# Storing the last two result tiles of a batched 64x64 matmul whole and in halves, instead of in halves and quarters

## The chip, the cores and the metric

One core of one Trainium2 chip. The metric is device time in microseconds (us), the median of the fast runs of a kernel. A core has a matrix engine (PE), a vector engine (DVE), a scalar engine (ACT), POOL and SP, which both mostly issue transfers here, and 16 transfer (DMA) engines that all issuers share.

## The reference

1024 independent products of 64x64 float32 matrices; 32 MB are read, 16 MB are written.

```python
def setup_inputs():
    return {
        "a": np.random.randn(1024, 64, 64).astype(np.float32),
        "b": np.random.randn(1024, 64, 64).astype(np.float32),
    }

def reference(a, b):
    return np.matmul(a, b).astype(np.float32)
```

## The kernel before

Sixteen steps t of 64 matrices each. A step casts b to bf16, spreads a's transposed blocks into a block-diagonal tile, multiplies into PSUM, copies the result to a 1 MB tile `o_sb` (128 partitions x 8 KB) and stores it. POOL issues all stores. The parts that matter, cut:

```python
n_t, n_s = B // 64, B // 128
HOLD = 2
o_v = out.rearrange("(t gh x) (mo w) n -> t (x mo) gh (w n)", gh=8, x=8, w=4)
o_pool = ctx.enter_context(tc.tile_pool(name="o_pool", bufs=8))
...
def store(t):
    for piece in held.pop(t):
        piece()

def multiply(t):
    ...
    last = t == n_t - 1
    o_sb = o_pool.tile([128, 8, 2, 2, 64], fp32, name="o_sb")

    def put(lo, n):                      # n of 8 parts: 8 is 1 MB, 4 is 512 KB, 2 is 256 KB
        nc.gpsimd.dma_start(
            out=o_v[t, :, lo : lo + n, :],
            in_=o_sb[:, lo : lo + n].rearrange("p gh j wl n -> p (gh j wl n)"),
        )
    ...                                  # matmuls; copies to o_sb after each half of the tile
                                         # (after each quarter of it in the last step)
    if last:
        held[t] = [lambda q=q: put(2 * q, 2) for q in range(4)]
    else:
        whole = t < n_t - 2
        held[t] = [lambda q=q: put(q, 8 if whole else 4) for q in ([0] if whole else [0, 4])]
...
for t in range(n_t):
    ...
    multiply(t)
    ...
    if t >= HOLD - 1:
        store(t - HOLD + 1)
for t in range(n_t - HOLD + 1, n_t):
    store(t)
```

Parts of 256 columns (1 KB per partition) are counted by `gh`. In the last step quarters 0 and 2 are copied by ACT, 1 and 3 by DVE. A store starts as soon as POOL reaches it and its copies have reported.

## Time and profile before

| | before |
|---|---|
| time, median of 3 | 135.43 us (135.34 to 135.49) |
| span in the profile | 133.8 us |
| busy: DVE, ACT, PE, POOL | 71%, 66%, 49%, 29% |
| transfers | 45.01 MB, mean 336 GB/s |
| last result copy done | 121.37 us |
| last transfer landed | 132.32 us |
| end | 133.77 us |

The time is from the runs; the next three rows are on the page of the profile; the last three are single records of the trace, in us from the span's start. Between the last copy and the last landing lie 11 us in which no engine computes.

"Landing" is the moment at which the sixteenth of the 16 transfer engines has reported a transfer as done. "Share" is the mean busy share of these 16 engines; it is a sum over packet records, and a full queue of POOL's stores shows as 1.01 to 1.04.

### The profile page before, as it was taken

To read this page: it belongs to the slowest core of one execution; us is meant where nothing else is said; L and a number is where in the kernel's file an instruction comes from. 1 tells how busy PE (TensorE), PEld (TensorE's weight loads), DVE (VectorE), ACT (ScalarE), POOL (GpSimd) and SP (SyncE) were. 2 spreads that over 40 slices of the span, in tenths; PEclk is the share of its full clock that TensorE was granted. 3 is DMA by queue.
4 is the path that set the end of the run, shared out by engine and by line. 5 is a ranking of instruction groups with operands and counts; after the bars stand their busy time and mean duration, and the time that the engine had idled before them with its cause. 6 is when DMAs were issued, how large, how long until landed. Compare 5 with 4: busy or idle time off the path is not lost.

```text
span 133.8 us, 2832 instructions
## 1 busy us (share of the span) xinstructions
PE 65.7 (49%) x1152; PEld 62.7 (47%) x1152; DVE 94.6 (71%) x120; ACT 87.7 (66%) x161; POOL 38.5 (29%) x49
## 2 busy tenths in 40 slices
PE   0007307970077463749919744991876376640000
PEld 0007207970077353649909744991866266630000
DVE  5930499108997059999999999899959989992000
ACT  3225424998038996758998985899793987992000
POOL 8991000420091080334124042003301220637000
PEclk9999999999559999555996896589677775797555
DMA  3999999999999999999999999999999999999991
GB/s 75 376 331 311 306 315 311 307 301 309 306 307 382 366 312 309 388 397 397 317 304 352 399 392 377 314 307 364 398 385 391 392 401 398 404 388 353 338 334 42
DMA packets 17485, 45.01 MB, mean 336 GB/s; under 512 B 1088, under 2 KB 1088, under 8 KB 17472
## 3 DMA queue, kind: packets, MB, share of 16 engines
q0 software_dynamic: 7440, 22.28, 54.8%
q1 hardware_dynamic: 5520, 13.11, 27.0%
q10 hardware_dynamic: 4512, 9.44, 18.6%
q8 instruction: 9, 0.15, 0.4%
q14 instruction: 4, 0.03, 0.1%
HBM read 33.55 MB, written 16.78 MB: 376 GB/s over the span
## 4 chain that ended last, share of the span: by engine, by line
DMA 35%; SPq 27%; DVE 15%; issue 6%; ACT 3%; POOL 3%; PE 3%; POOLq 1%; DVEq 0%; ACTq 0%
SPq L72 22%; DMA a_raw<-in_a_dram 18%; DMA b_sb<-in_b_dram 17%; DVE at_bd L128 8%; DVE b_bf L139 5%; SPq L91 3%; POOL out_dram L161 3%; PE o_ps L184 3%; ACT o_sb L172 2%; DVE o_sb L172 1%; SPq L85 1%; ACT b_bf L146 1%; DVE a_bf L106 1%; DVE a_bf L103 1%; POOLq L278 1%
## 5 line engine op out<-in xcount | busy, mean ns | idle before, releaser
L172 ACT COPY o_sb<-o_ps 64x512 f32<-64x512 f32 x106 | 61.6, 581 | 14.3 <-PE o_ps L184 13.0
L184 PEld LDWEIGHTS <-at_bd 128*128 128x128 bf16 x1024 | 41.6, 111 | 34.9 <-DVE b_bf L139 22.4
L184 PE MATMUL o_ps<-b_bf,at_bd 128*128 128x64 bf16 x960 | 41.9, 215 | 31.1 <-DVE b_bf L139 20.9
L128 DVE COPY at_bd<-at_sb 32x1024 f32<-32x1024 f32 x64 | 46.0, 719 | 13.4 <-ACT at_sb L118 11.6
L161 POOL DMA_DIRECT2D out_dram<-o_sb x20 | 20.6, 1031 | 58.1 <-ACT o_sb L172 21.4
L115 PE MATMUL at_ps<-identity,a_bf 128*128 128x128 f32 x128 | 23.4, 360 | 20.6 <-ACT a_bf L100 11.0
L115 PEld LDWEIGHTS at_ps<-identity,a_bf 128*128 128x128 f32 x128 | 21.6, 196 | 20.8 <-issue 19.3
L118 ACT COPY at_sb<-at_ps 128x512 f32<-128x512 f32 x32 | 16.9, 596 | 8.2 <-PE at_ps L115 8.0
L68 POOL DMA_DIRECT2D a_sb<-in_a_dram x21 | 13.9, 673 | 25.9 <-DVE a_bf L103 19.9
L139 DVE CAST b_bf<-b_sb 128x2048 bf16<-128x2048 f32 x14 | 17.4, 1245 | 2.9 <-DMA b_sb<-in_b_dram 2.6
L172 DVE COPY o_sb<-o_ps 64x512 f32<-64x512 f32 x14 | 9.7, 690 | 0.6 <-ACT o_sb L172 0.3
L106 DVE CAST a_bf<-a_raw 128x1024 bf16<-128x1024 f32 x7 | 5.5, 792 | 5.7 <-DMA a_raw<-in_a_dram 5.7
L103 DVE COPY a_bf<-a_sb 128x3072 bf16<-128x3072 bf16 x7 | 7.0, 1006 | 0.0
L100 ACT CAST a_bf<-o_sb 128x1024 bf16<-128x1024 f32 x2 | 2.1, 1044 | 5.0 <-DMA o_sb<-in_a_dram 5.0
L139 ACT CAST b_bf<-b_sb 128x2048 bf16<-128x2048 f32 x1 | 1.9, 1898 | 3.8 <-DMA b_sb<-in_b_dram 3.8
L100 DVE CAST a_bf<-o_sb 128x1024 bf16<-128x1024 f32 x2 | 2.8, 1380 | 1.9 <-DMA o_sb<-in_a_dram 1.9
L212 DVE MEMSET at_bd<- 128x4096 f32 x1 | 3.5, 3472 | 0.8 <-issue 0.8
L172 DVE COPY o_sb<-at_ps 64x256 f32<-64x256 f32 x8 | 3.4, 422 | 0.3 <-PE at_ps L184 0.2
L172 ACT COPY o_sb<-at_ps 64x256 f32<-64x256 f32 x8 | 2.9, 367 | 0.1
L209 ACT ACT_TABLE_LOAD x1 | 1.3, 1283 | 2.3 <-issue 2.3
L184 PE MATMUL at_ps<-b_bf,at_bd 128*128 128x64 bf16 x64 | 2.0, 193 | 1.2 <-DVE at_bd L128 1.2
L217 POOL MEMSET at_bd<- 128x2048 f32 x1 | 1.8, 1849 | 0.0
(12 smaller groups left out, 5.5 us busy)
## 6 DMA issues: line engine op xcount, KB each, us to landing
out_dram<-o_sb POOLq DMA_DIRECT2D x14, 1024.0 KB, 23.6
a_sb<-in_a_dram POOLq DMA_DIRECT2D x21, 256.0 KB, 17.4
a_raw<-in_a_dram SPq DMA_DIRECT2D x7, 512.0 KB, 24.2
o_sb<-in_a_dram ACTq DMA_DIRECT2D x2, 512.0 KB, 7.0
o_sb<-in_a_dram SPq DMA_DIRECT2D x2, 512.0 KB, 5.9
out_dram<-o_sb POOLq DMA_DIRECT2D x2, 512.0 KB, 11.4
out_dram<-o_sb POOLq DMA_DIRECT2D x4, 256.0 KB, 10.1
b_sb<-in_b_dram SPq DMA_DIRECT2D x8, 0.5 KB, 22.2
```

What stands on the lines that cost most here:

```text
L68: nc.gpsimd.dma_start(out=a_sb[:, h, :, :].rearrange("p v k -> p (v k)"), in_=a_v[s, h])
L72: nc.sync.dma_start(out=a_raw[:].rearrange("p v k -> p (v k)"), in_=a_v[s, 3])
L100: copy(a_bf[:, :, h, :], a_sb[h].rearrange("p (v k) -> p v k", v=16))
L103: nc.vector.tensor_copy(a_bf[:, :, 0:3, :], cast_sb[:].rearrange("p h v k -> p v h k"))
L106: nc.vector.tensor_copy(a_bf[:, :, 3, :], raw[:])
L115: nc.tensor.transpose(at_ps[:, vo, :], a_cols[:, 4 * vo + 2 * j + wl, :], identity[:])
L118: nc.scalar.copy(at_tiles[s][:, j, :, wl, :, :], at_ps[:].rearrange("p vo (g mp) -> p g mp vo", mp=4),)
L128: nc.vector.tensor_copy(bd[rows, :, :, :, h, :].rearrange("p j g wl mo -> p j (g wl) mo"), at_tiles[t // 2][rows, :, half, :, :, :].rearrange(
L139: (nc.vector.tensor_copy if t else nc.scalar.copy)(b_bf[:], b_sb[:])
L161: nc.gpsimd.dma_start(out=o_v[t, :, lo : lo + n, :], in_=o_sb[:, lo : lo + n].rearrange("p gh j wl n -> p (gh j wl n)"),)
L172: copies[2 * par + wl](dst, src)
L184: nc.tensor.matmul(o_ps[:, gl, g % 2, j, :], at_bd[:, j, g, :, u], b_bf[:, g, 64 * u : 64 * u + 64], start=(u == 0), stop=(u == 1),)
```

## The change

The last two tiles are cut more coarsely: three stores in place of six. The bytes and the copies are the same. The intent of the fine cut had been to start the last stores early and to leave little to move after the last copy; the intent of the change is fewer transfers.

```diff
-        if last:
-            held[t] = [lambda q=q: put(2 * q, 2) for q in range(4)]
-        else:
-            whole = t < n_t - 2
-            held[t] = [lambda q=q: put(q, 8 if whole else 4) for q in ([0] if whole else [0, 4])]
+        held[t] = [lambda q=q: put(q, 4) for q in (0, 4)] if last else [lambda: put(0, 8)]
```

## The prediction

> **What bounds the kernel now.** The change touches only how the results of the last two of sixteen steps are cut into stores, so I read the profile from its end backwards: the busy slices, the last 18 us by windows, the issues of the stores with their time to landing, the copies that feed them, and the exit.
>
> The page's row of slices first (each 3.3 us): the DMA engines are full from the second slice to the last but one.
>
> ```profile
> DMA  3999999999999999999999999999999999999991
> GB/s 75 376 331 311 306 315 311 307 301 309 306 307 382 366 312 309 388 397 397 317 304 352 399 392 377 314 307 364 398 385 391 392 401 398 404 388 353 338 334 42
> ```
>
> The stretch in question, busy time by windows (columns: stretch, its length, then PE, weight load, DVE, ACT and POOL busy with counts, granted clock, DMA share of 16 engines, GB/s):
>
> ```profile
> 116.00:120.00 4.00, 2.04 (x64) 1.92 (x64) 3.67 (x9) 3.88 (x9) 1.68 (x2) 1.00 1.02 389
> 120.00:124.00 4.00, 0.00 (x0) 0.00 (x0) 1.06 (x3) 1.34 (x4) 2.85 (x4) 0.78 1.01 355
> 124.00:128.00 4.00, 0.00 (x0) 0.00 (x0) 0.00 (x0) 0.00 (x0) 0.00 (x0) 0.50 1.02 344
> 128.00:130.00 2.00, 0.00 (x0) 0.00 (x0) 0.00 (x0) 0.00 (x0) 0.00 (x0) 0.50 0.96 338
> 130.00:131.00 1.00, 0.00 (x0) 0.00 (x0) 0.00 (x0) 0.00 (x0) 0.00 (x0) 0.50 0.56 213
> 131.00:132.00 1.00, 0.00 (x0) 0.00 (x0) 0.00 (x0) 0.00 (x0) 0.00 (x0) 0.50 0.10 41
> ```
>
> All computing is over before 122 us; the transfer engines work on at a share of 1.0 until nearly 130. They never pause in the stretch in which the affected stores are issued: at the end the kernel is a queue of stores being emptied. The timeline of that stretch, with the two kinds of copies and POOL's issues:
>
> ```profile
> 113.58 4.74 ACT L172 COPY o_sb<-o_ps 64x512 f32<-64x512 f32 x8 [0.70 <-PE o_ps L184]
> 113.83 1.35 POOL L161 DMA_DIRECT2D out_dram<-o_sb  x1 [4.22 <-ACT b_bf L146]
> 116.23 0.92 POOL L161 DMA_DIRECT2D out_dram<-o_sb  x1 [1.05 <-ACT o_sb L172]
> ...
> 117.59 3.49 DVE L172 COPY o_sb<-at_ps 64x256 f32<-64x256 f32 x8 [0.22 <-PE at_ps L184]
> 118.34 3.03 ACT L172 COPY o_sb<-at_ps 64x256 f32<-64x256 f32 x8
> 118.61 0.75 POOL L161 DMA_DIRECT2D out_dram<-o_sb  x1 [1.46 <-ACT o_sb L172]
> 120.14 2.96 POOL L161 DMA_DIRECT2D out_dram<-o_sb  x4 [0.77 <-ACT o_sb L172]
> ```
>
> In order: step 13 whole (113.83), step 14 in halves (116.23 and 118.61), step 15 in four quarters (from 120.14). How long each waits in the queue is in the list of DMA issues, taken in windows that hold one of them, at 113.5, 116, 118.5 and 121.6 us (KB, then us from issue to landing):
>
> ```profile
> out_dram<-o_sb POOLq DMA_DIRECT2D x1, 1024.0 KB, 12.7
> ...
> out_dram<-o_sb POOLq DMA_DIRECT2D x1, 512.0 KB, 11.9
> ...
> out_dram<-o_sb POOLq DMA_DIRECT2D x1, 512.0 KB, 11.0
> ...
> out_dram<-o_sb POOLq DMA_DIRECT2D x1, 256.0 KB, 10.0
> ```
>
> A 256 KB transfer takes under 0.8 us of the queue's time at 340 GB/s, yet lands 10 us after its issue: over 9 us are the transfers ahead of it. Last, what all that is made of, the DMA part from 119.9 us to the end:
>
> ```profile
> DMA packets 1043, 3.76 MB, mean 267 GB/s; under 512 B 128, under 2 KB 128, under 8 KB 1041
> q0 software_dynamic: 1041, 3.74, 76.0%
> ```
>
> The 128 small ones are semaphore updates, 16 for each of the 8 transfers that land after 119.9 us. The other 913 are all of 4096 bytes: in the packet records quarters, halves and whole stores are cut alike.
>
> **What the Trainium skill says.** "DMA: Bandwidth & Descriptors", section "Anatomy of one DMA — SWDGE (gpsimd) path", puts a fixed cost of about 2.0 us on each such transfer and says that it is mostly completion latency. The trace agrees that it is latency and not occupancy: the four quarters land at 130.33, 131.03, 131.68 and 132.32 us (the landing records), 0.64 to 0.70 us apart, which is the bytes alone (the working is below). The same page, "Rules for kernel authors", says of two transfers to disjoint halves that they serialize on the same engines. The landing records agree: the halves of step 14 land at 128.08 and 129.62, one after the other. "Perfetto Trace Analysis", section "DMA Optimizations", says that splitting may help if the DMA engines are generally idle; here, at a share of 1.01 to 1.02, they aren't. The same page, "DMA Instruction — SWDGE (GPSIMD)", says that the profiled end of such an issue is the end of writing descriptors and not of the transfer; 0.71 us of POOL against 10 us to landing agrees.
>
> **The change part by part.** Six stores become three; bytes, order and copies stay.
>
> *Step 14.* The store of the first half at 116.23 goes. The whole store waits for the second half's copies, done at 118.32 (113.58 + 4.74), so it is issued where the second half is now, at 118.61, with some 0.9 to 1.4 us of POOL (whole stores take 0.90 and 1.35 at 108.71 and 113.83) in place of 0.75. It holds back 512 KB by 2.4 us. Does the queue run dry? Step 13's store lands at 113.83 + 12.7 = 126.5 on the slowest engine; its landing record has the fastest of the 16 engines done at 123.42. The descriptors of step 14 are complete by 118.61 + 1.4 = 120.0. So the fastest engine has 3.4 us left in hand, the slowest 6.5. Cost: 0.
>
> *Step 15.* By the copies' own records the first quarter is ready at 119.85 (ACT), the second at 119.32 (DVE), the third at 121.37 (ACT), the fourth at 121.08 (DVE). The first half can be issued when the first quarter is now, 120.14; the second 0.30 us after 121.37, at 121.67. Now POOL issues four of 0.71 and finishes at 123.09; after, with two of some 0.75 to 0.92 (the rows of the halves), the last descriptor is written by about 122.6, 0.5 us earlier. Step 14 was not landed on the fastest engine until 126.36. So the 0.5 us meet a queue that is over 3.5 us long: gain 0.
>
> *Work of the transfer engines.* The payload is the same 4096-byte packets: 0.76 x 16 x 14.1 us / 913 gives 0.188 us each, and steps 14 and 15 are 2 MB = 512 packets, 32 for each engine, whichever way they are cut. Check: from step 13's landing (126.50) to the last (132.32) are 5.82 us, or 0.182 us for each of 32. A quarter is 4 packets per engine, 0.64 to 0.70 us by the landings, 0.16 to 0.18 each, no dearer than a half's 8 in 1.54 (0.19): no gap per transfer is visible. What goes are the semaphore updates of three transfers, one per engine and transfer of 9 ns (packet records): 3 x 0.009 = 0.03 us gained.
>
> *The exit.* From the last landing (132.32) to the end (133.77) pass 1.45 us. At the exit SP waits for the transfers' semaphores one after another, 0.06 us each, in a fixed order that starts near the last-but-one of POOL's eight semaphores and comes to the first of them, on which the last quarter lands now, late: five steps remain after that landing, and SP is through at 132.63. Transfers take the eight in turn. With three fewer, I expect the last half on the sixth, the second in SP's list: some ten steps then follow the last landing, 5 x 0.06 = 0.3 us more, SP through at about 132.9. But POOL's own drain ends only at 132.98, and the barrier follows it at 133.03, so this should just hide. I count +0.05 us for it, a choice between 0 and 0.3.
>
> Sum: 0 + 0 - 0.03 + 0.05, about +0.02 us on 135.43: I predict 135.4 us.
>
> **The rivals.**
>
> *The transfer engines run dry* because 512 KB come 2.4 us later. If nothing were queued, that would cost the 512 KB at 390 GB/s, 1.3 us (136.8). Against it: a share of 1.02 throughout 116 to 120 us, and 11 to 13 us from issue to landing.
>
> *Fewer transfers save fixed cost.* Three times the skill's 2 us, were it serial, would give 129.4; even 0.3 us each would give 134.5. Against it: the landings 0.64 to 0.70 us apart, which leave no room beside the bytes.
>
> *A coarse last piece is exposed.* If the last store's own time set the end, 512 KB in place of 256 KB would add a quarter's 0.64 to 0.70 us (136.1). For it: this is the usual reason for a finer last piece. Against it: it would need a last issue that meets an empty queue, and it meets over 9 us of work.
>
> *POOL becomes faster and the end follows.* 0.5 us less of POOL's issuing would give 134.9 if the issue set the end. The chain of waits on the page does run through these POOL issues, but it ends with POOL's sequencer at 122.38, over 9 us before the last landing: it follows POOL's order and not the transfers, so I don't take its word.
>
> *Another order of packets, another rate.* A quarter's packets gather other rows than a half's, and packets take 0.165 us at 110 to 118 us and 0.18 to 0.20 from 119 to 129, for a reason that I can't read from this trace (whole stores and halves alike are slow there). If the 32 packets per engine went at 0.165, the end would come 32 x 0.017 = 0.5 us earlier; at 0.19, 0.26 us later. This is the widest honest uncertainty.
>
> **Range and chances.** From the rate -0.5 to +0.26, from the exit 0 to +0.3, runs spread by 0.15 us (135.34 to 135.49): 134.95 to 135.85. Two per cent are 2.7 us, and no rival that the profile leaves standing reaches half of that. Faster by over 2%: 0.01; within 2%: 0.98; slower by over 2%: 0.01.
>
> **What would show it right or wrong.** Right: the DMA share stays at 1.0 from 116 to 129 us; POOL's last issue ends near 122.6, yet the last landing is within 0.5 us of 132.3; the half that comes last lands over 9 us after its issue, and the two halves land about 1.3 to 1.5 us apart; small packets after 119.9 us are 80 in place of 128 (5 transfers x 16); POOL's drain still ends after SP's last wait. Wrong: a share under 0.9 between 118 and 126 us (ran dry), a last landing a full 0.65 us later at the same rate (exposed piece), one over 1 us earlier (fixed costs), or an exit longer than 1.45 us by 0.3 (the order of SP's waits).

## The result

| | before | changed |
|---|---|---|
| time, median | 135.38 us (135.33 to 135.49, 4 runs) | 135.49 us (135.35 to 135.53, 4 runs) |
| span in the profile | 133.8 us | 133.6 us |
| last result copy done | 121.37 us | 123.08 us |
| last store's issue starts | 122.37 us | 123.63 us |
| last transfer landed | 132.32 us | 132.25 us |
| from there to the end | 1.45 us | 1.39 us |

The ratio is 1.0005, with a 95% interval of 0.9988 to 1.0022: no difference.

The windows of the changed kernel that answer to those of before (same columns):

```profile
116.00:120.00 4.00, 2.83 (x54) 2.67 (x52) 2.75 (x5) 3.87 (x8) 1.22 (x2) 0.50 1.02 392
120.00:124.00 4.00, 1.26 (x24) 1.10 (x21) 2.97 (x8) 1.87 (x6) 1.21 (x3) 0.50 1.01 358
124.00:128.00 4.00, 0.00 (x0) 0.00 (x0) 0.00 (x0) 0.00 (x0) 0.38 (x1) 0.50 1.02 341
128.00:130.00 2.00, 0.00 (x0) 0.00 (x0) 0.00 (x0) 0.00 (x0) 0.00 (x0) 0.50 0.94 334
130.00:131.00 1.00, 0.00 (x0) 0.00 (x0) 0.00 (x0) 0.00 (x0) 0.00 (x0) 0.50 0.59 225
131.00:132.00 1.00, 0.00 (x0) 0.00 (x0) 0.00 (x0) 0.00 (x0) 0.00 (x0) 0.50 0.12 49
```

The share of the transfer engines (last column but one) is what it was to within 0.03, window by window. The columns of the computing engines are not: in 120 to 124 us PE, DVE and ACT are busy for 1.26, 2.97 and 1.87 us, where before it was 0.00, 1.06 and 1.34. The timeline of the changed kernel says the same:

```profile
117.67 3.59 PE L184 MATMUL at_ps<-b_bf,at_bd 128*128 128x64 bf16 x64 [1.17 <-DVE at_bd L128]
118.91 3.03 ACT L172 COPY o_sb<-at_ps 64x256 f32<-64x256 f32 x8
119.18 0.89 POOL L161 DMA_DIRECT2D out_dram<-o_sb  x1 [2.78 <-ACT o_sb L172]
119.59 3.49 DVE L172 COPY o_sb<-at_ps 64x256 f32<-64x256 f32 x8 [1.19 <-PE at_ps L184]
121.87 0.77 POOL L161 DMA_DIRECT2D out_dram<-o_sb  x1 [1.80 <-DVE o_sb L172]
123.63 0.75 POOL L161 DMA_DIRECT2D out_dram<-o_sb  x1 [0.99 <-issue]
```

In this execution the computing ran 1.7 us later at its end. The granted clock was 0.50 in 116 to 124 us, against 1.00 and 0.78 in the two windows of before, and the last step's matmuls took 3.59 us where they took 2.04 us before (the trace of before, same group). This is not the change's doing: 1.2 us of it are there before the first store that differs (116.23 us), as DVE's last spreading copies (L128) start at 114.52 us and not at 113.30; and with the finer cut below the last copy ended late too, at 123.07 us. That the clock is the cause is likely, not shown. But it is a useful accident: the last copy and the last issue came 1.7 and 1.3 us later, and the last landing did not move (132.25 against 132.32).

The issues of steps 14 and 15 of the changed kernel with their time to landing, each in a window that holds it alone:

```profile
out_dram<-o_sb POOLq DMA_DIRECT2D x1, 1024.0 KB, 10.4
...
out_dram<-o_sb POOLq DMA_DIRECT2D x1, 512.0 KB, 9.1
...
out_dram<-o_sb POOLq DMA_DIRECT2D x1, 512.0 KB, 8.6
```

At 340 GB/s a half needs 1.5 us of the queue. With little or nothing ahead, halves landed 4.2 to 5.3 us after their issue (the runs without a queue, below), so some 3 to 5 of these 8.6 to 9.1 us go by behind what is ahead. And the packets after 119.9 us:

```profile
DMA packets 999, 3.78 MB, mean 268 GB/s; under 512 B 80, under 2 KB 80, under 8 KB 997
q0 software_dynamic: 997, 3.76, 76.2%
```

The small ones have gone from 128 to 80, three transfers x 16, and the share is 76.2% against 76.0%: the work of the transfer engines is the same.

### The profile page after: what moved, and what is told of

It reads as the page before. It is cut to its first block, busy times and chain, and to the rows that moved or that the text cites. A ratio compares the mean times of both kernels' runs of the same rounds, so it can differ in the third digit from the quotient of the medians.

```text
span 133.6 us, 2826 instructions
## 1 busy us (share of the span) xinstructions
PE 66.0 (49%) x1152; PEld 62.6 (47%) x1152; DVE 94.5 (71%) x120; ACT 87.5 (65%) x161; POOL 36.9 (28%) x46
## 4 chain that ended last, share of the span: by engine, by line
DMA 34%; DVE 22%; SPq 16%; PE 7%; ACT 7%; issue 5%; POOLq 1%; ACTq 1%; DVEq 0%
DMA b_sb<-in_b_dram 34%; SPq L72 14%; DVE at_bd L128 10%; ACT o_sb L172 7%; DVE o_sb L172 6%; DVE b_bf L139 4%; PE o_ps L184 3%; PE at_ps L115 3%; SPq L91 2%; PE at_ps L184 1%; DVE a_bf L106 1%; DVE a_bf L103 1%; SPq L85 1%; POOLq L274 1%; ACTq L91 1%
## 5 line engine op out<-in xcount | busy, mean ns | idle before, releaser
L184 PEld LDWEIGHTS <-at_bd 128*128 128x128 bf16 x1024 | 43.0, 113 | 37.5 <-DVE b_bf L139 22.3
L128 DVE COPY at_bd<-at_sb 32x1024 f32<-32x1024 f32 x64 | 46.0, 719 | 13.4 <-ACT at_sb L118 11.7
L161 POOL DMA_DIRECT2D out_dram<-o_sb x17 | 19.1, 1121 | 61.5 <-ACT o_sb L172 21.9
L115 PE MATMUL at_ps<-identity,a_bf 128*128 128x128 f32 x128 | 21.9, 343 | 20.8 <-ACT a_bf L100 11.1
L115 PEld LDWEIGHTS at_ps<-identity,a_bf 128*128 128x128 f32 x128 | 20.1, 185 | 21.0 <-issue 19.5
L184 PE MATMUL at_ps<-b_bf,at_bd 128*128 128x64 bf16 x64 | 3.6, 242 | 1.2 <-DVE at_bd L128 1.2
```

What stands on the lines that cost most here:

```text
L115: nc.tensor.transpose(at_ps[:, vo, :], a_cols[:, 4 * vo + 2 * j + wl, :], identity[:])
L128: nc.vector.tensor_copy(bd[rows, :, :, :, h, :].rearrange("p j g wl mo -> p j (g wl) mo"), at_tiles[t // 2][rows, :, half, :, :, :].rearrange(
L161: nc.gpsimd.dma_start(out=o_v[t, :, lo : lo + n, :], in_=o_sb[:, lo : lo + n].rearrange("p gh j wl n -> p (gh j wl n)"),)
L184: nc.tensor.matmul(o_ps[:, gl, g % 2, j, :], at_bd[:, j, g, :, u], b_bf[:, g, 64 * u : 64 * u + 64], start=(u == 0), stop=(u == 1),)
```

## The experiments

The theory: at the end the kernel is a full queue of stores, so how the last two are cut, and when they are issued, doesn't count as long as the queue doesn't run dry. The rivals: each transfer has a fixed cost; a coarse last piece is exposed; the end follows POOL's issues. In each diff "-" is the changed kernel, unless said otherwise. Four kernels ran together in each of the first two groups and three in the last, each group with its own runs of before (135.45, 135.47 and 135.55 us).

### Coarser still: both whole

```diff
-        held[t] = [lambda q=q: put(q, 4) for q in (0, 4)] if last else [lambda: put(0, 8)]
+        held[t] = [lambda: put(0, 8)]
```

> Both last stores whole, 1 MB each (five stores fewer than before's eight pieces had counted from step 14 on: two in place of six). Theory of the full queue: the last store is still issued over 3 us before the slowest transfer engine has worked off what lies ahead, so the time stays within 0.4 us of 135.4. Rival, exposed last piece: 1 MB in place of 256 KB at the end adds three quarters of 0.65 us, so about 2 us (137.4). Rival, fixed cost per transfer: earlier by 0.3 us or more for each of four transfers saved (134.2 or less).

(Six pieces become two, so four fewer; the "five" in the expectation is a slip.) Measured: 135.25 us (6 runs), ratio to before 0.9988, interval 0.9972 to 1.0004. The last store, of 1 MB, was issued at 123.15 us and landed at 132.14. The exposed piece would have cost 2 us, the fixed cost would have given 1.2 us or more back; neither came. Its issue, and the windows of the queue after it:

```profile
123.15 0.89 POOL L161 DMA_DIRECT2D out_dram<-o_sb  x1 [3.53 <-issue]
...
122.00:126.00 4.00, 0.00 (x0) 0.00 (x0) 0.59 (x2) 0.00 (x0) 0.89 (x1) 0.50 1.01 350
126.00:130.00 4.00, 0.00 (x0) 0.00 (x0) 0.00 (x0) 0.00 (x0) 0.00 (x0) 0.50 0.98 342
```

### Finer: both in quarters

```diff
-        held[t] = [lambda q=q: put(q, 4) for q in (0, 4)] if last else [lambda: put(0, 8)]
+        held[t] = ([lambda q=q: put(q, 2) for q in (0, 2, 4, 6)] if t >= n_t - 2
+                   else [lambda: put(0, 8)])
```

> Both last stores in quarters, eight transfers in place of six. Full queue: within 0.4 us of 135.4; more small packets after 120 us (16 for each transfer). Fixed cost per transfer: later by 0.3 us or more for each of two transfers (136.0 or more). Finer is better: earlier than before by 0.3 us or more.

Measured: 135.61 us (6 runs), ratio 1.0016, interval 1.0000 to 1.0032. Same again. One detail: the last quarter could be issued only at 127.06 us, 3.4 us after the one before it. POOL's transfers take eight semaphores in turn, and the transfer eight places ahead of it, step 13's store, landed at 126.52. Even so late an issue, 4.7 us later than the last one of before, landed at 132.28, with the rest of the queue:

```profile
123.63 0.71 POOL L161 DMA_DIRECT2D out_dram<-o_sb  x1 [1.30 <-DMA out_dram<-o_sb]
127.06 0.72 POOL L161 DMA_DIRECT2D out_dram<-o_sb  x1 [2.73 <-DMA out_dram<-o_sb]
...
126.00:130.00 4.00, 0.00 (x0) 0.00 (x0) 0.00 (x0) 0.00 (x0) 0.72 (x1) 0.50 0.98 333
```

Each run's own interval reaches 1, but between themselves the two differ: five of the six runs with two pieces lie under all six with eight, and the ratios are 0.28% (0.38 us) apart, of which the profiles show 0.20 us in the exit (below). So a cost of some 0.06 us per piece is not excluded, though six and three pieces do not show it; the rival's 0.3 us is excluded.

### Holding stores back until the queue must run dry

The control of the theory: it has to fail when the queue is empty. POOL reads a word of each of the last copies before it issues the stores of steps 13 to 15 (or 12 to 15). The results stay right.

```diff
+        if last:
+            held["o_sb"] = o_sb
...
-            if t >= HOLD - 1:
+            if HOLD - 1 <= t < 13 + HOLD - 1:
                 store(t - HOLD + 1)
-        for t in range(n_t - HOLD + 1, n_t):
+        for gh in (4, 6):
+            nc.gpsimd.tensor_copy(warm[:, 0:1], held["o_sb"][:, gh, 1, 1, 63:64])
+        for t in range(13, n_t):
             store(t)
```

> As the changed kernel, but POOL reads a word of the last copies before it issues the stores of steps 13, 14 and 15, so that all three are held back until the last copy is done (about 121.5 to 123 us). Full queue: step 12's store lands on the slowest engine at 123.7 to 123.9, and the first packets of step 13 come about 1.3 us after the last copy, at 122.8 to 124.4: the queue is just used up on the slowest engine, so 0 to 1.0 us later than 135.4. Rival, the end follows the issues: 3 stores of 0.75 to 1.35 us in a row after the last copy, and the end moves by the delay of step 13's issue, 6 to 8 us.

Measured: 137.99 us (6 runs from 137.29 to 138.72), ratio 1.0187, interval 1.0153 to 1.0222. Later by 2.5 us where 0 to 1.0 was expected: the expectation missed. Two of its terms were too small. The last copy ended at 122.72 us, POOL's issue started at 123.70 and the first packet of step 13 went at 125.16, so 2.4 us and not 1.3 from copy to packet. The other is the pause. Step 12 had landed on its slowest engine at 123.66 but on its fastest at 120.95 us, so the transfer engines stood still for 1.5 to 4.2 us, 3.3 on the mean of the 16 landing records (121.85); the expectation had looked at the slowest alone. What followed was slower by 1.0 us: 9.87 us from the first packet to the mean of the last landings (135.03), where before took 8.87 from step 12's mean landing (122.12) to the end of the same three stores (130.99). Slower packets (0.197 us against 0.187) give 0.01 x 48 packets per engine = 0.5 us; some 0.35 more is the time from the last packet's end (135.00) to its landing, which counts at one end only here. Together 3.3 + 1.0, less the 0.3 us by which step 12 landed earlier: 4.0 us on the mean engine. The last landing of this profile (135.35) is late by only 3.03 us, since the 16 engines finished within 0.7 us, and within 3.0 us in before. The rival fared no better: issued 9.9 us later than before, step 13 delayed the last landing by 3.0 us in the profile (135.35 against 132.32), not by 6 to 8.

> The same with steps 12 to 15 held back. Full queue: step 11 lands on the slowest engine at 119.9 to 120.3, the first packets of step 12 come at 122.8 to 124.4, so every engine stands still for 2.5 to 4.5 us and the end comes that much later (138 to 140). A dip of the DMA share near 121 to 123 us must show it. Should it stay at 135.4, the theory of the queue is wrong.

Measured: 141.71 us (6 runs), ratio 1.0445, interval 1.0413 to 1.0477: 6.3 us later, where 2.5 to 4.5 was expected; right in kind, again too small: step 11 had landed at 119.95 us on the slowest engine and at 119.12 on the mean, and the first packet of step 12 went at 125.30, a pause of 5.3 us for the slowest and 6.2 for the mean. The windows of this run show the hole in the queue:

```profile
116.00:120.00 4.00, 3.09 (x59) 2.93 (x57) 2.72 (x7) 3.87 (x9) 0.00 (x0) 0.50 0.68 266
120.00:122.00 2.00, 0.46 (x14) 0.34 (x11) 1.95 (x5) 1.57 (x5) 0.18 (x1) 0.99 0.00 0
122.00:124.00 2.00, 0.00 (x0) 0.00 (x0) 0.49 (x2) 0.00 (x0) 0.36 (x2) 0.86 0.00 0
124.00:126.00 2.00, 0.00 (x0) 0.00 (x0) 0.00 (x0) 0.00 (x0) 2.00 (x3) 0.50 0.36 123
126.00:130.00 4.00, 0.00 (x0) 0.00 (x0) 0.00 (x0) 0.00 (x0) 1.97 (x3) 0.50 1.00 310
```

From 120 to 124 us the transfer engines moved nothing (share 0.00). The kernel is that sensitive to late stores; it just isn't at the two stores that the change delays.

### The queue taken away: the same cut made to matter

The stores of steps 4 to 13 are left out (a wrong result), once with the cut of before, once with that of the changed kernel.

```diff
-        for piece in held.pop(t):
+        pieces = held.pop(t)
+        if 4 <= t < n_t - 2:
+            return
+        for piece in pieces:
             piece()
```

> Wrong on purpose: the stores of steps 4 to 13 are left out (10 MB), so that no queue stands ahead of the last two stores; steps 14 and 15 are cut as in the kernel before (halves, quarters). The span should fall to 105 to 120 us, and the last piece should land 2 to 3 us after its issue in place of 10.

> Wrong on purpose, the same stores left out, steps 14 and 15 cut as in the changed kernel (whole, halves). Full queue: with the queue taken away the coarser cut is exposed, and it ends 0.3 to 1.5 us later than short_before (the whole store of step 14 starts some 2.4 us later, and the last piece has a quarter's 0.65 us more of data). Fixed cost or POOL's issuing as the true limit: it ends earlier than short_before, by 0.5 us or more.

Measured: 127.70 us with the cut of before, 128.78 with the changed one (6 runs each). Against the same runs of before the ratios are 0.9433 and 0.9499, so the changed cut is 0.9499 / 0.9433 = 1.007 times as long, 0.9 us: as expected of the queue, and against both rivals. (The 0.9 us are the difference of the means, 0.3 to 1.5 by the scatter of the 6 runs each; that of the medians is 1.1.) The span fell less than I expected (to 125.5 and 126.9 us and not 105 to 120): the last copy still ended at 120 us, so it is not mainly the stores that time it. The stores with the fine cut, from the timeline, then with the coarse one:

```profile
113.98 0.88 POOL L164 DMA_DIRECT2D out_dram<-o_sb  x1 [51.37 <-ACT o_sb L175]
116.39 0.77 POOL L164 DMA_DIRECT2D out_dram<-o_sb  x1 [1.53 <-ACT o_sb L175]
116.54 3.49 DVE L175 COPY o_sb<-at_ps 64x256 f32<-64x256 f32 x8 [1.12 <-PE at_ps L187]
117.91 2.24 POOL L164 DMA_DIRECT2D out_dram<-o_sb  x3 [0.76 <-ACT o_sb L175]
120.32 0.72 POOL L164 DMA_DIRECT2D out_dram<-o_sb  x1 [0.17 <-issue]
```

```profile
116.37 0.92 POOL L164 DMA_DIRECT2D out_dram<-o_sb  x1 [53.42 <-ACT o_sb L175]
116.57 3.48 DVE L175 COPY o_sb<-at_ps 64x256 f32<-64x256 f32 x8 [1.19 <-PE at_ps L187]
118.87 0.78 POOL L164 DMA_DIRECT2D out_dram<-o_sb  x1 [1.59 <-DVE o_sb L175]
120.60 0.75 POOL L164 DMA_DIRECT2D out_dram<-o_sb  x1 [0.94 <-issue]
```

DVE's last copy ends at 120.03 and 120.05 us, so the comparison is fair. With the fine cut POOL starts storing at 113.98, with the coarse one at 116.37, and the last landings are at 123.35 and 124.92 us. Each of these transfers lands 3.0 to 5.3 us after its issue, where the same pieces took 8.6 to 12 with the queue ahead. So the fine cut does what it was made for, but only where transfers are not queued up at the end.

### Do late packets go slower because of where they write?

Packets take 0.165 us at 110 to 118 us and 0.18 to 0.20 from 119 to 130. Step t writes to the place of step 15 - t (wrong).

```diff
-                out=o_v[t, :, lo : lo + n, :],
+                out=o_v[n_t - 1 - t, :, lo : lo + n, :],
```

> Wrong on purpose: step t's results go to the place of step 15 - t; nothing else differs from the changed kernel. It asks why packets take 0.165 us at 110 to 118 us and 0.18 to 0.20 from 119 to 129. If it goes by the place in HBM: the last stores go at about 0.165 and the end comes some 0.5 us earlier. If it goes by the moment: packets slow down at 118 to 119 us as before, time within 0.4 us of 135.4.

Measured: one look, 135.50 us (state unknown, as for any single run). The windows 110 to 118 and 122 to 126 us show 401 and 347 GB/s, as in before (403 and 347). So, by this one look, it isn't the place in HBM. Nor does the moment alone seem to decide: in the run with steps 13 to 15 held back, where no store is issued between step 12's and 123.70 us, packets took 0.166 us at 118 to 119 us and 0.172 at 119 to 120, the queue still full, where in before it was 0.175 and 0.180. What it is stays open: the stores that run without a queue ahead of them go at 0.19 us per packet from the start (the two runs above), and so do those after the hole in the run with steps 12 to 15 held back.

### SP in place of POOL for the last stores

```diff
-            nc.gpsimd.dma_start(
+            (nc.sync if last else nc.gpsimd).dma_start(
```

> The two halves of step 15 are issued from SP in place of POOL. Full queue: another queue on the same transfer engines, the same bytes: within 0.4 us of 135.4, but these halves land earlier (the two queues take turns) and steps 13 and 14 later. If POOL's descriptors or its drain at the exit set the end: earlier by 0.3 us or more.

Measured: 134.92 us (6 runs from 134.62 to 134.93), ratio 0.9952, interval 0.9939 to 0.9965. Half a per cent faster, a little beyond what the queue alone allows, and what the expectation named for POOL's drain. The last landing is at 131.75 us (before: 132.32), and the exit takes 1.09 us (before: 1.45). The exit can be read. The two drains of interest, from the exit's instructions of before, and then of this run (line numbers differ, since the kernels do; columns: count, shortest, median and longest in ns, first and last start in us):

```profile
L278 POOLq DRAIN  x3: 51/102/10828, 122.2 to 133.5; - x3
```

```profile
L274 POOLq DRAIN  x3: 51/93/11182, 119.1 to 132.6; - x3
```

Before, POOL's long drain starts at 122.15 and takes 10.83 us, to 132.98: 0.66 us beyond the last landing. SP had been through with its waits at 132.63, so the barrier, at 133.03, waited for POOL. With the last step on SP, POOL's drain starts at 119.13 and is over at 130.31, long before the last landing, and the barrier follows SP at 132.10. That accounts for 0.36 us of the gain. (Against the changed kernel, from which this one differs in nothing else, the exit is shorter by 0.30.) Why the last landing itself came earlier by 0.57 us is not shown, and the profile is of the fastest of the six runs, 134.62 us, 0.3 under their median, so part of it may be scatter; the packets were no faster (1024 bytes each on SP's queue, 47.8 ns, which is 191 ns for 4096).

Is it the exit, or are stores from SP better as such? Three more kernels, with steps 14 and 15, 12 to 15 and 9 to 15 issued from SP (`t >= 14`, `t >= 12`, `t >= 9` in place of `last`):

> After the run with step 15 stored from SP came out about 0.5 us faster than before (0.3 of it in the exit, where POOL's drain had ended 1.5 us before the last landing, the rest in an earlier last landing): here step 14 (whole) and step 15 (halves) are both issued from SP. If only POOL's drain at the exit was in the way, there is nothing more to gain: within 0.2 us of that run, 134.7 to 135.1. If stores from SP go through the transfer engines faster as such, a 1 MB store more on SP gains again as much in the landing: 134.3 to 134.6.

> Steps 12 to 15 from SP. Exit alone: 134.7 to 135.1, as with one or two steps. Stores from SP faster as such: 133.5 to 134.3, and the DMA part shows over 360 GB/s from 120 to 128 us, where it is 340 to 355 now.

> Steps 9 to 15 from SP, all of those whose turn comes after SP's last load. Exit alone: 134.7 to 135.1. Stores from SP faster as such: under 133.5. A loss is possible too: more packets of 1024 bytes in place of 4096; if those cost more each, the time goes over 135.4.

| stored from SP | time | ratio to before (95%) | last landing | exit |
|---|---|---|---|---|
| step 15 | 134.92 us | 0.9952 (0.9939 to 0.9965) | 131.75 us | 1.09 us |
| steps 14, 15 | 134.71 us | 0.9940 (0.9924 to 0.9957) | 131.97 us | 1.04 us |
| steps 12 to 15 | 134.81 us | 0.9949 (0.9936 to 0.9962) | 132.05 us | 1.27 us |
| steps 9 to 15 (5 runs) | 135.49 us | 0.9999 (0.9987 to 1.0011) | 132.10 us | 1.22 us |

One, two or four steps gain much the same, 0.5 to 0.8 us; a gain in time that grew with the bytes is excluded, and the landing moved by no more than 0.6 us in any. Yet the rate that an expectation had named as the sign of faster stores, over 360 GB/s from 120 to 128 us, did come: 350 in before, 357 with one or two steps from SP, 367 with four, 383 with seven. With seven the rate was lower earlier (383 at 110 to 118 us, where POOL's stores went at 403). So in these single profiles the rate goes with the issuer, or with its smaller packets; why the landing hardly gains is not shown. With seven steps all of it is gone, though the profile has the span at 133.3 us, shorter than before (133.8): its profiled execution took 135.46 us, 2.1 us more than the span, where before it is 1.8 (135.55 and 133.8), and the other four runs show the same 2.0 to 2.1 us. What the loss is stays open. Storing steps 14 and 15 from SP is the fastest version found, 0.6% under before.

### POOL's drain over the runs

From the trace of each run, the time from the last landing of a POOL store to the end of POOL's drain, by the number of pieces into which steps 14 and 15 were cut: 2 pieces 0.49 us, 3 pieces 0.53, 6 pieces 0.66, 8 pieces 0.75; without a queue, 3 pieces 1.18 and 6 pieces 1.31. In both rows a piece more goes with some 0.043 us more. This is a regularity over six single profiles and not a tested cause; and with steps 12 to 15, or 9 to 15, from SP it was 1.39 and 1.27 us although SP's stores were queued, so an empty queue is not all that goes with the longer drain.

## Why the prediction was right

*What bounds the end.* Right, and shown: three cuts with two, three and eight pieces time within 0.3% of before, a last issue as late as 127.06 us still landed at 132.28, and when the queue was made to run dry the time rose by 2.5 and 6.3 us.

*Step 14, cost 0.* Right. Its whole store was issued at 119.18 us and done with at 120.07; step 13 was not landed on its fastest engine until 123.62.

*Step 15, gain 0 from POOL's earlier end.* The conclusion held, the numbers in it did not. POOL's last issue ended at 124.38 us and not near 122.6. One part is the later computing of that execution; another is that the second half waits for DVE's copy, after which POOL started 0.55 us later (123.08 to 123.63), where I had taken the 0.30 us that it needed after ACT's copy before. So the last half landed 8.6 us after its issue, under the 9 that I had named as a sign, and the two halves landed 1.27 us apart (130.98 and 132.25), just under the 1.3 named. None of it reached the end, because the queue ahead was long enough. The sign itself was badly chosen: the prediction puts over 9 of a quarter's 10 us down to the transfers ahead, but with no queue a quarter still took 3.0 to 3.3 us from issue to landing, so about 7 us were the queue.

*Work of the transfer engines.* Right: 32 packets per engine took 5.91 us from step 13's landing (126.34 to 132.25), 0.185 us each against 0.182, and the small packets went from 128 to 80 as counted.

*The exit.* The mechanism was right, the balance was not. The last half did land on the sixth semaphore, and SP had ten steps left: through at 132.87 us, 0.62 after the landing. But POOL's drain, which I had expected to stay behind SP's last wait, ended at 132.78, sooner after the landing (0.53 us) than before (0.66). So SP's list set the end by 0.09 us, and the exit came out at 1.39 us in place of 1.45, where I had added 0.05.

*The rivals.* The fixed cost per transfer and the exposed piece are excluded here, at the sizes that they named, by the whole and the quartered cut; the exposed piece is real, 0.9 us, once the queue is gone. The predicted +0.02 us came out as a ratio of 1.0005 that can't be told from 1; so close a hit is partly luck: the exit alone came out 0.11 us off, within the scatter of the runs. The widest uncertainty, the packet rate, did not move between the two. And the upper end of the stated range, 135.85, is not the sum of its own terms: 135.43 + 0.26 + 0.3 is 135.99. It did not matter here.

## What to carry to other kernels

Before cutting a last store finer, compare how long it takes from issue to landing with what it takes with nothing ahead: here 10 us against 3.0, so the queue covered some 7 us, and its size and its issue could not matter; they mattered at once (0.9 us) when nothing was queued ahead. When the transfers are the last thing to end, look at what comes after the last landing as well: whose drain and which list of waits the end goes through. Issuing the last one to four stores from another engine than the one with the long drain gained half a per cent here, more than any way of cutting them.

## What the Trainium skill lacked or had wrong

- "DMA: Bandwidth & Descriptors", "Anatomy of one DMA — SWDGE (gpsimd) path": its fit, 2.0 us + bytes / 436 GB/s, gives 2.6 us for 256 KB (an estimate from the page). With no queue ahead such stores took 3.0 to 3.3 us from issue to landing; with a queue, four in a row landed 0.64 to 0.70 us apart. The fixed part is latency, as the page says, and costs nothing in a full queue.
- The same page, "Specifications": a first byte after some 1 us for this kind of transfer. From the start of the issue to the first packet 1.45 to 1.49 us were measured, in the four runs that issued into an empty queue; from which moment the page counts, it does not say.
- The same page, "Issuing engines are not separate DMA queues", says that issuing from several engines only saves the sequencer's time. The last landing agrees (within 0.6 us whoever issued); but the choice of issuer was worth 0.5 to 0.6%, part of it through the exit, and with more stores from SP the rate at 120 to 128 us rose from 350 to 383 GB/s (single profiles).
- No page that I read describes the program's own exit as seen here (L278 in before): SP's waits for all transfer semaphores in a fixed order, 0.06 us each, and POOL's drain, over 0.41 to 0.75 us after POOL's last store has landed in nine profiles and 1.18 to 1.39 us in four (the two without a queue, and steps 12 to 15 or 9 to 15 from SP).
- No page explains why packets of 4096 bytes took 0.165 us at 110 to 118 us and about 0.19 later; the place in HBM is excluded by one look, and with steps 13 to 15 held back packets still took 0.166 us at 118 to 119.
